# RWKV-7 mixer in a decoder step: preparation of a pair of heads split over two blocks, and the tensor engine's products kept in written order

## Chip, cores and metric

The kernel runs on one core of a Trainium2 chip. The metric is the device time of one execution in microseconds (us). The program is fully unrolled: there are no loops left on the chip, and each engine runs one fixed list of instructions.

## What is computed

One inference step of a two-layer decoder: 256 prompt tokens and 8 samples of 4 tokens, 288 columns in all. Layer 0 mixes with Mamba-2, layer 1 with RWKV-7; around each mixer stand two SwiGLU networks and a gate. The change is in the RWKV-7 mixer, whose core for each of 16 heads of width 64 is a recurrence over time:

```python
def step(S, inp):
    r_t, d_t, k_t, v_t, kk_t, a_t = inp
    sa = jnp.einsum('bhij,bhj->bhi', S, -kk_t)
    S = (S * d_t[:, :, None, :] + sa[..., None] * (kk_t * a_t)[:, :, None, :]
         + v_t[..., None] * k_t[:, :, None, :])
    return S, jnp.einsum('bhij,bhj->bhi', S, r_t)
```

Before it stand projections of the mixed rows (r, k, v, and low-rank ones for decay, a and the gate g), after it a group norm, a bonus term, the gate and the projection `w_o`.

## The kernel before

**Engines and weights.** Weights come from memory in units of 128x1024 (tile `raw`, issued on SP). Four 128x128 tiles at a time are split into a high part (`whi`, ACT, L55) and a low part (`wlo`, DVE, L56); the pool `wsp` holds 8 such pieces of each. A product of a weight tile with 288 columns is three matmuls (`mm3`, L147 to L149). The projection of k is one fp32 matmul a tile (L1134), recorded as two.

**Pairs and chunks.** The 16 heads are 8 pairs; a pair fills the 128 partitions. The tokens of a pair are 5 chunks of 64 columns: four of the prompt, one with the samples. Within a chunk the recurrence becomes a triangular system, which is inverted by levels.

**Three generators make the stage.** Each `yield` ends a step.

- `prep(p)`, 18 steps s1 to s18: s1 squares k and sums it over a head (L1228: two products with `ones_m`), exponentials of the summed decay; s2 scales k, r and kk into the tiles `BK` and `AR` (13 DVE operations, no matmul); s3 and s4 the products between tokens (`by_tokens`, L1265) into `AA` and `BKt`; s5 the matrices `N16`, `XT` and a transpose; s6 to s15 five levels of two steps each: `Z` (L1325), then `X` and `XT` (one or two groups of products in `mms`, L1309); s16 to s18 a refinement, whose result is `TT`. s16 is read by ACT (`X0`) and by DVE (`IX`, L1348).
- `chain(p)`, 17 steps c1 to c17: c1 the bonus (two products) and 16 products with the samples' states `S0` (L1383); c2 to c13 `solve`, `solved` and `state` for the four prompt chunks in turn, with the samples' chunk beside them in c5, c6, c8 (`masked`) and c10 (`samples`); c14 splits the output `y`; c15 and c16 are two products each with `center` and `ones_m` (group norm); c17 ends it.
- `bulk(p)` and `bulk2(p)`, the large products of a pair, in items: `bulk2` g (five matmuls), then v in eight items, then the transpose of v (`pv`, L1180); `bulk` the decay and a (`sw`, `sa`), then k in eight items and r in eight. 27 items in all.

**Blocks and rounds.** The stage is written as blocks p = 0 to 8. Block p runs `chain(p - 1)` and `prep(p)` in rounds; in each round every generator does one step, and then 1.45 items on average (`RATE`) come from `fill(p)`: `bulk2(p)` and `bulk(p + 1)`, at the start also the gate's first layer (`gates`), at the end products of `w_o`.

```python
        for p in range(KD + 1):
            gens, acc = [], 0.0
            bulk = fill(p)
            if p < KD:
                gens.append(w.prep(p))
            if p > 0:
                gens.insert(0, w.chain(p - 1))
```

**What sets the order.** When the program is built, a scheduler lays out each engine's list. It keeps data dependences and buffers, and by its own estimate of times it lets an instruction that is ready pass an earlier one of the same engine that is not. So the tensor engine's order is not the written one.

**Buffers.** PSUM has eight banks, dealt out in rings (`set_rings`): `main` [0, 1, 7] for the large products, `A` [2, 3] for `prep` and `pv`, `R` [4, 5] and `Y` [6] for `chain`. A new group of products takes the ring's next bank when that bank's readers have ended.

Of the kernel before, what the change touches and what calls it, by code (L numbers as in the profile page):

```python
# [78 lines left out]
class K:  # L79
    def __init__(self, tc, io):  # L80
        self.tc, self.nc, self.io = tc, tc.nc, io
        self.la_split, self.la_units = 16, 4
        self.lagged = []
        self.bg = []
        self.uid = 0
        self.ring_at = {}
        self.act_set, self.act_load, self.act_group = None, None, []
# [55 lines left out]

    def mm3(self, ps, w, x, start, stop):
        nc = self.nc
        (wh, wl), (xh, xl) = w, x
        nc.tensor.matmul(ps, wh, xh, start=start, stop=False)  # L147
        nc.tensor.matmul(ps, wh, xl, start=False, stop=False)  # L148
        nc.tensor.matmul(ps, wl, xh, start=False, stop=stop)  # L149
# [801 lines left out]
RATE = 1.45  # L951
# [42 lines left out]
class Rwkv:  # L994
# [50 lines left out]
    def lead(self, g, r):  # L1045

        nc, k, ws = self.nc, self.k, self.k.ws
        so = self.t("so", [P, KD, 9])
        pu, pw = k.bank("main")[:, :NT], k.bank("main")[:, :NT]
        k.renew(8, 16, F32)  # L1050
        hg = k.A[8:16]
        for kt in range(KD):
            k.act(hg[kt], k.h[kt], AF.Copy, scale=g[:, kt:kt + 1])
            w = k.wn.next_whole("r_wa1", kt, 0)
            nc.tensor.matmul(pu, w, hg[kt], start=kt == 0, stop=kt == KD - 1)
        for kt in range(KD):
            nc.vector.tensor_tensor(self.u[kt], hg[kt], r, ALU.mult)
        lw = k.tmp("s")
        nc.vector.tensor_tensor(lw, pu, r, ALU.mult)
        for kt in range(KD):  # L1060
            u, xx = self.u[kt], self.xx[kt]
            us, xs = s84(u[:, 256:288]), s84(xx[:, 256:288])
            nc.vector.tensor_tensor(xx[:, 1:288], u[:, 0:287], u[:, 1:288], ALU.subtract)
            nc.vector.tensor_tensor(xs[:, :, 0:1], k.sh[:, kt].rearrange("p (b o) -> p b o", o=1), us[:, :, 0:1],
                                    ALU.subtract)
            k.act(xx[:, 0:1], u[:, 0:1], AF.Copy, scale=-1.0)
            nc.tensor.matmul(pw, k.sc[kt], xx, start=kt == 0, stop=kt == KD - 1)
            k.act(so[:, kt, 0:1], u[:, 255:256], AF.Copy)
            k.act(so[:, kt, 1:9].rearrange("p (b o) -> p b o", o=1), us[:, :, 3:4], AF.Copy)
        nc.sync.dma_start(k.io["shift_o"], so)  # L1070
        nc.vector.tensor_tensor(lw, lw, pw, ALU.add)
        k.act(lw[0:64], lw[0:64], AF.Tanh)
        self.stack(self.lw, lw, slice(0, 64), slice(64, 128))
        self.stack(self.la, lw, slice(64, 128), slice(0, 64))

    def gates(self):

        nc, k = self.nc, self.k
        pg = [k.bank(n)[:, :NT] for n in "YR"]
        for kt in range(KD):  # L1080
            m = [None] * kt + [self.t("mg", bufs=2)]
            self.mix(5, kt, m)
            for i in range(2):
                nc.tensor.matmul(pg[i], k.wn.next_whole("r_g1", kt, i), m[kt], start=kt == 0, stop=kt == KD - 1)  # L1084
# [13 lines left out]
    def stacked(self, ps, w, x, start=True):  # L1098

        self.nc.tensor.matmul(ps, w[0], x, start=start, stop=False)  # L1100
        self.nc.tensor.matmul(ps, w[1], x, start=False, stop=True)
# [24 lines left out]
    def proj(self, n, i, x, p):  # L1126

        k, d = self.k, self.d[p]
        ps = k.bank("main")[:, :NT]
        for kt in range(KD):  # L1130
            if p == 0:
                self.mix(i, kt, x)
            if n == "k":
                self.nc.tensor.matmul(ps, k.wn.next_whole("r_wk", kt, p), x[kt], start=kt == 0, stop=kt == KD - 1)  # L1134
# [27 lines left out]
    def bulk2(self, p):  # L1162
# [6 lines left out]
        d["g"] = self.t("g", bufs=3)  # L1169
# [7 lines left out]
        for ch in range(5):  # L1177
            for h in range(2):
                rows = slice(64 * h, 64 * h + 64)
                nc.tensor.matmul(pv[rows, 64 * ch:64 * ch + 64], v[rows, 64 * ch:64 * ch + 64] if ch < 4 else V[rows],  # L1180
                                 self.I[rows], start=True, stop=True)
# [5 lines left out]
    def mm2(self, ps, m, hi, lo):  # L1187

        self.nc.tensor.matmul(ps, m, hi, start=True, stop=False)  # L1189
        self.nc.tensor.matmul(ps, m, lo, start=False, stop=True)  # L1190
# [8 lines left out]
    def pads(self):  # L1199
        self.AR = [self.t(f"AR{i}", [P, 5, 2, 64]) for i in range(2)]  # L1200
# [14 lines left out]
    def prep(self, p):  # L1215
# [4 lines left out]
        AR, BK = self.AR[p % 2], self.BK  # L1220
        d["S0"] = self.t("S0", [P, 8, 64], bufs=2)
        nc.sync.dma_start(d["S0"], k.io["wkv_in"][p])
# [25 lines left out]
        rk = d["rk"] = self.t("rk", bufs=2)  # L1248
# [8 lines left out]
        AA = d["AA"] = self.t("AA", [P, 2, 5, 128], bufs=2)  # L1257
        BKt = d["BKt"] = self.t("BKt", [P, 2, 5, 64], bufs=2)
        H = [(h, slice(64 * h, 64 * h + 64), slice(64 - 64 * h, 128 - 64 * h)) for h in range(2)]

        def by_tokens(ps, ch, o, n, rhs):

            for i in (1, 0):
                for h, rows, ro in H:
                    nc.tensor.matmul(ps[h][rows if i else ro, o:o + n], BK[rows, ch, i], rhs(rows), start=True, stop=True)  # L1265
# [21 lines left out]
        N16 = self.t("N16", [P, 5, 64], F16)  # L1287
# [12 lines left out]
        X, XT = [self.t(n, [P, 5, 64], F16, bufs=2) for n in ("X", "XT")]  # L1300
        nc.vector.tensor_tensor(XT, N16, lv(0, 5), ALU.mult)

        def mms(lhs, rhs, n=5):

            ps = k.bank("A")[:, :320].rearrange("p (c t) -> p c t", c=5)
            for ch in range(n):
                for h in range(2):
                    rows = slice(64 * h, 64 * h + 64)
                    nc.tensor.matmul(ps[rows, ch], lhs(ch)[rows], rhs(ch)[rows], start=True, stop=True)  # L1309
# [11 lines left out]
        for i in range(1, 6):  # L1321
            n = chunks(i)
            pz = mms(at(N16), at(X), n)
            Z = self.t("Z", [P, 5, 64], F16)
            nc.vector.tensor_tensor(Z[:, :n], pz, lv(i, n), ALU.mult)  # L1325
            yield
            if i < 5:
                px = mms(at(XT), at(Z), n)
                X2 = self.t("X", [P, 5, 64], F16, bufs=2)
                k.act(X2[:, :n], px, AF.Copy)  # L1330
            pt = mms(at(Z), at(XT), n)
            XT2 = self.t("XT", [P, 5, 64], F16, bufs=2)
            k.act(XT2[:, :n], pt, AF.Copy)
            X, XT = X2, XT2
            if i == 1:
                XTs = self.t("XTs", [P, 64], F16)
# [6 lines left out]

        ps = mms(full, eye)
# [6 lines left out]
        for ch in range(5):  # L1351
            for h in range(2):
                rows = slice(64 * h, 64 * h + 64)
                nc.tensor.matmul(ps[rows, ch], AA[rows, 1 - h, ch, 0:64], X0[rows, ch], start=True, stop=True)
# [9 lines left out]
    def chain(self, p):  # L1364
# [4 lines left out]
        AR, AA, BKt, SAV, TT, E1, S0 = self.AR[p % 2], d["AA"], d["BKt"], d["SAV"], d["TT"], d["E1"], d["S0"]  # L1369
# [11 lines left out]
        for b in range(8):  # L1381
            for h, rows, _ in H:
                nc.tensor.matmul(pq[rows, 8 * b:8 * b + 8], S0[rows, b], AR[rows, 4, 0, 8 * b:8 * b + 8], start=b == 0,  # L1383
# [6 lines left out]
        def solve(ch):  # L1390

            pr, S = k.bank("R"), st["S"]
            for h, rows, ro in H:
                if ch == 4:
                    nc.tensor.matmul(pr[ro, 0:64], q[rows], self.I[rows], start=True, stop=False)
                elif S is not None:
                    nc.tensor.matmul(pr[ro, 0:64], AR[rows, ch, 0], S[rows], start=True, stop=False)
            for h, rows, ro in H:
                nc.tensor.matmul(pr[ro, 0:64], AA[rows, h, ch, 0:64], SAV[rows, h, ch], start=ch < 4 and S is None,
                                 stop=True)  # L1400
            if ch < 4 and S is not None:
                for h, rows, _ in H:
                    nc.tensor.matmul(py[rows, 64 * ch:64 * ch + 64], S[rows], AR[rows, ch, 1], start=False, stop=True,
# [4 lines left out]
        def solved(ch):  # L1408
            ps, S, rhs = k.bank("R"), st["S"], st[ch]
            for h, rows, _ in H:  # L1410
                nc.tensor.matmul(ps[rows, 0:64], TT[rows, ch], rhs[rows], start=True, stop=True)
# [6 lines left out]
        def state(ch):  # L1418
# [3 lines left out]
            for h, rows, _ in H:  # L1422
                nc.tensor.matmul(ps[rows, 0:64], BKt[:, h, ch], SAV[:, h, ch], start=True, stop=True)  # L1423
# [6 lines left out]
            for h, rows, _ in H:  # L1430
                nc.tensor.matmul(o[rows], SAV[:, h, ch], AA[:, h, ch, 64:128], start=False, stop=True,
# [12 lines left out]
        def samples():  # L1444

            ps = k.bank("R")
            for h, rows, _ in H:
                nc.tensor.matmul(pq[rows], SAV[:, h, 4], AA[:, h, 4, 64:128], start=False, stop=True,
                                 skip_group_check=True)
            for h, rows, _ in H:  # L1450
                nc.tensor.matmul(ps[rows, :], BKt[:, h, 4], st["sv"][h].rearrange("p b i -> p (b i)"), start=True,  # L1451
# [42 lines left out]
def rwkv(k, g, g_next):  # L1494
# [3 lines left out]
    with k.tc.tile_pool(name="rwkv", bufs=1) as pool:  # L1498
# [6 lines left out]
        k.set_rings(main=[0, 1, 7], A=[2, 3], R=[4, 5], Y=[6])  # L1505
# [17 lines left out]
        def fill(p):  # L1523
# [11 lines left out]
            if p == KD:  # L1535
# [220 lines left out]
```

## Time and profile before

| what | value |
|---|---|
| median of 3 runs | 1533.58 us (1533.34 to 1533.81) |
| the profiled execution's own time | 1533.7 us |
| its span, first to last instruction | 1531.7 us |
| granted tensor-engine clock, mean | 0.996 |
| blocks of the RWKV stage | from about 985 to about 1285 us of the span |
| in them: PE, weight loads, DVE, ACT busy | 295.1, 223.8, 224.0, 191.0 of 300 us |

PE is the tensor engine's matmuls, PEld its weight loads, DVE the vector engine, ACT the scalar engine. A row of the timeline gives the start in us from the span's start, the duration, engine, line, operation, the tiles (out<-in), the shape and, with xN, how many like instructions were merged; a bracket at the end is idle time of the engine before it and what ended that. Matmuls are pipelined, so durations of neighbours overlap: the distance between starts tells what one costs.

### The profile page before, as it was taken

The numbers are of one execution on the slowest core, as the hardware profiler recorded it, in microseconds if no ns is written. First come the engines' busy times: TensorE is split into PE (matmuls) and PEld (weight loads), VectorE is DVE, ScalarE is ACT, GpSimd is POOL, SyncE is SP. The second block draws the span as 40 slices with busy tenths as digits, with TensorE's granted clock in tenths as the row PEclk, the third lists the DMA queues.
The fourth block names the chain that finished last, engine by engine and source line by source line (L and its number), as shares of the span: only waits on it lengthen the run. The fifth ranks groups of instructions, "written<-read, shape, count | busy, mean of one in ns | idle before, by whom it ended". The sixth has DMA issues, their size and how long they took to land.

```text
span 1531.7 us, 35590 instructions
## 1 busy us (share of the span) xinstructions
PE 1512.1 (99%) x14178; PEld 1420.4 (93%) x14178; DVE 1099.8 (72%) x2321; ACT 970.4 (63%) x2217; POOL 48.5 (3%) x145
## 2 busy tenths in 40 slices
PE   9999999999999999999999999999999999999997
PEld 9999999999999999999999999777677778999997
DVE  7666568999998666656876655887776778666666
ACT  7555458999996555555755554766666746555545
POOL 0000002112100000000000000100000000000000
PEclk9999999999999999999999999999999999999999
DMA  7555563776765555555555555532222225555551
GB/s 246 167 167 166 169 208 118 260 237 204 249 227 188 172 166 166 166 166 168 168 166 166 167 165 167 163 111 71 76 74 66 71 65 163 166 166 166 167 169 56
DMA packets 75574, 243.48 MB, mean 159 GB/s; under 512 B 11728, under 2 KB 16976, under 8 KB 75408
## 3 DMA queue, kind: packets, MB, share of 16 engines
q1 hardware_dynamic: 75408, 241.21, 49.4%
q8 instruction: 111, 1.82, 0.5%
q14 instruction: 55, 0.45, 0.1%
HBM read 226.54 MB, written 14.64 MB: 157 GB/s over the span
## 4 chain that ended last, share of the span: by engine, by line
PE 92%; DVE 4%; ACT 3%; DMA 1%; issue 1%; SPq 0%; POOL 0%; DVEq 0%; POOLq 0%; ACTq 0%
PE bank L147 26%; PE bank L149 26%; PE bank L148 25%; PE bank L1309 2%; PE bank L1134 1%; PE bank L772 1%; PE bank L1451 1%; PE bank L1423 1%; PE bank L776 1%; PE bank L768 1%; PE bank L1189 1%; DVE wlo L56 1%; PE bank L1383 1%; PE bank L1084 1%; PE bank L749 0%
## 5 line engine op out<-in xcount | busy, mean ns | idle before, releaser
L147 PE MATMUL bank<-act,whi 128*128 128x288 f32 x2760 | 823.2, 299 | 5.8 <-ACT act L138 3.9
L148 PE MATMUL bank<-act,whi 128*128 128x288 f32 x2760 | 819.6, 297 | 0.9 <-DVE act L156 0.9
L149 PE MATMUL bank<-act,wlo 128*128 128x288 f32 x2760 | 815.2, 296 | 0.1
L55 ACT ACTIVATE whi<-raw 128x512 fp32r<-128x512 f32 x754 | 472.3, 632 | 434.4 <-PE bank L148 422.7
L56 DVE TENSOR_TENSOR wlo<-raw,whi 128x512 fp32r<-128x512 f32 x754 | 515.4, 689 | 262.8 <-ACT whi L55 236.0
L147 PEld LDWEIGHTS bank<-act,whi 128*128 128x128 f32 x2760 | 517.6, 188 | 11.9 <-ACT act L138 5.5
L148 PEld LDWEIGHTS bank<-act,whi 128*128 128x128 f32 x2760 | 521.9, 189 | 5.9 <-DVE act L156 1.8
L149 PEld LDWEIGHTS bank<-act,wlo 128*128 128x128 f32 x2760 | 521.2, 189 | 2.8 <-DVE wlo L56 0.3
L147 PE MATMUL bank<-more,whi 128*128 128x288 f32 x192 | 56.7, 295 | 0.0
L148 PE MATMUL bank<-more,whi 128*128 128x288 f32 x192 | 56.5, 294 | 0.0
L149 PE MATMUL bank<-more,wlo 128*128 128x288 f32 x192 | 56.4, 294 | 0.0
L321 DVE TENSOR_TENSOR t<-bank,rstd 128x288 f32<-128x288 f32 x88 | 39.8, 456 | 23.0 <-PE bank L149 23.0
L324 DVE TENSOR_TENSOR u<-bank,s 128x288 f32<-128x288 f32 x88 | 39.8, 456 | 22.6 <-PE bank L149 22.6
L673 DVE SCALAR_TENSOR_TENSOR conv_a<-X,vec,conv_a 128x312 f32<-128x312 f32 x96 | 50.9, 534 | 3.8 <-ACT conv_a L138 3.4
L138 ACT ACTIVATE s<-t 128x288 f32<-128x288 f32 x104 | 45.8, 443 | 6.1 <-DVE t L366 3.5
L138 ACT ACTIVATE X<-bank 128x256 f32<-128x256 f32 (+2 forms) x98 | 30.7, 340 | 21.8 <-PE bank L1309 20.8
L138 ACT ACTIVATE act<-h,vec 128x288 fp32r<-128x288 f32 (+1 forms) x71 | 37.1, 528 | 7.4 <-DMA h<-in_xT 2.8
L1134 PE MATMUL bank<-act,raw 128*128 128x288 f32 x128 | 40.8, 434 | 0.0
L148 PEld LDWEIGHTS bank<-more,whi 128*128 128x128 f32 x192 | 36.3, 189 | 0.0
L149 PEld LDWEIGHTS bank<-more,wlo 128*128 128x128 f32 x192 | 36.2, 189 | 0.0
L147 PEld LDWEIGHTS bank<-more,whi 128*128 128x128 f32 x192 | 36.0, 187 | 0.0
L1325 DVE TENSOR_TENSOR Z<-bank,lv 128x256 f16<-128x256 f32 (+1 forms) x40 | 17.5, 437 | 24.0 <-PE bank L1309 23.5
(385 smaller groups left out, 1737.1 us busy)
## 6 DMA issues: line engine op xcount, KB each, us to landing
raw<-in_w SPq DMA_DIRECT2D x377, 512.0 KB, 3.6
h0a<-in_ssm_a SPq DMA_DIRECT2D x16, 512.0 KB, 5.7
h0b<-in_ssm_b SPq DMA_DIRECT2D x16, 512.0 KB, 5.1
out_ssm_s<-h0b SPq DMA_DIRECT2D x16, 512.0 KB, 4.3
raw<-in_wn SPq DMA_DIRECT2D x11, 512.0 KB, 3.5
S<-in_wkv_in SPq DMA_DIRECT2D x8, 256.0 KB, 3.9
out_wkv_s<-S SPq DMA_DIRECT2D x8, 256.0 KB, 2.0
h<-in_xT SPq DMA_DIRECT2D x8, 144.0 KB, 4.4
```

The source lines that it names most:

```text
L55: nc.scalar.activation(hi, src, AF.Copy)
L56: nc.vector.tensor_tensor(lo, src, hi.bitcast(F32), ALU.subtract)
L138: i = self.nc.scalar.activation(out, in_, func, **kw)
L147: nc.tensor.matmul(ps, wh, xh, start=start, stop=False)
L148: nc.tensor.matmul(ps, wh, xl, start=False, stop=False)
L149: nc.tensor.matmul(ps, wl, xh, start=False, stop=stop)
L321: nc.vector.tensor_tensor(t, pg, r, ALU.mult)
L324: nc.vector.tensor_tensor(u, pu, s, ALU.mult)
L673: nc.vector.scalar_tensor_tensor(a[:, :312], X[:, t:t + 312], k.g(f"conv_w{t}")[:, ct:ct + 1], a[:, :312], ALU.mult, ALU.add)
L1134: self.nc.tensor.matmul(ps, k.wn.next_whole("r_wk", kt, p), x[kt], start=kt == 0, stop=kt == KD - 1)
L1309: nc.tensor.matmul(ps[rows, ch], lhs(ch)[rows], rhs(ch)[rows], start=True, stop=True)
L1325: nc.vector.tensor_tensor(Z[:, :n], pz, lv(i, n), ALU.mult)
```

## The change

- A third pair is at work at once. `prep(p)` is cut in two: its first 9 steps (`HALF`) run in block p, the other 9 in block p + 1, and `chain(p)` runs in block p + 2. There are ten blocks, 0 to 9, and in a round the order is chain step, step of the older prep, step of the younger prep, items.
- From the first block to the last, each tensor-engine product goes through `K.mm`, which ties it behind the one written before it. The tie is for the scheduler alone: it puts no wait on the chip.
- `RATE` 1.45 becomes 1.6; `bulk2(p)` moves one block later.
- Rings: `main` [0, 1], `A` [2, 3, 7].
- Buffers: `AR`, `AA`, `BKt`, `rk` 3 instead of 2; `N16`, `Z` 2 instead of 1; `X`, `XT`, `XTs` one set for even and one for odd pairs; `mg` 1 instead of 2, `g` 2 instead of 3; `wsp` 6 instead of 8 for the whole kernel.
- The load of `S0` moves from s1 to s16.

```diff
+    def mm(self, *a, **kw):
+        i = self.nc.tensor.matmul(*a, **kw)
+        if self.kept is not None:
+            if self.kept:
+                self.after(i, self.kept[-1])
+            self.kept = [i]
+        return i
...
-RATE = 1.45
+RATE = 1.6
+HALF = 9
...
-            m = [None] * kt + [self.t("mg", bufs=2)]
+            m = [None] * kt + [self.t("mg", bufs=1)]
...
-        d["g"] = self.t("g", bufs=3)
+        d["g"] = self.t("g", bufs=2)
...
-        d["S0"] = self.t("S0", [P, 8, 64], bufs=2)
-        nc.sync.dma_start(d["S0"], k.io["wkv_in"][p])
...
+        d["S0"] = self.t("S0", [P, 8, 64], bufs=2)
+        nc.sync.dma_start(d["S0"], k.io["wkv_in"][p])
         ps = mms(full, eye)
...
-        k.set_rings(main=[0, 1, 7], A=[2, 3], R=[4, 5], Y=[6])
+        k.set_rings(main=[0, 1], A=[2, 3, 7], R=[4, 5], Y=[6])
...
-            if p < KD:
-                yield from w.bulk2(p)
+            if 0 < p <= KD:
+                yield from w.bulk2(p - 1)
             if p + 1 < KD:
                 yield from w.bulk(p + 1)
-            if p == KD - 1:
+            if p == KD:
...
-        for p in range(KD + 1):
+        preps = {}
+        k.kept = []
+        for p in range(KD + 2):
             gens, acc = [], 0.0
             bulk = fill(p)
+            if p > 1:
+                gens.append(w.chain(p - 2))
+            if 0 < p <= KD:
+                gens.append(preps.pop(p - 1))
             if p < KD:
-                gens.append(w.prep(p))
-            if p > 0:
-                gens.insert(0, w.chain(p - 1))
+                preps[p] = w.prep(p)
+                gens.append(itertools.islice(preps[p], HALF))
...
+        k.kept = None
...
-            tc.tile_pool(name="wsp", bufs=8) as k.wsp, \
+            tc.tile_pool(name="wsp", bufs=6) as k.wsp, \
```

More of the change, by code (lines that the diff above doesn't have):

```diff
@@ L1 @@
+import itertools
 import numpy as np
@@ L85, in __init__ @@
         self.uid = 0
+        self.kept = None
         self.ring_at = {}
@@ L1054, in lead @@
             w = k.wn.next_whole("r_wa1", kt, 0)
-            nc.tensor.matmul(pu, w, hg[kt], start=kt == 0, stop=kt == KD - 1)
+            k.mm(pu, w, hg[kt], start=kt == 0, stop=kt == KD - 1)
         for kt in range(KD):
@@ L1066, in lead @@
             k.act(xx[:, 0:1], u[:, 0:1], AF.Copy, scale=-1.0)
-            nc.tensor.matmul(pw, k.sc[kt], xx, start=kt == 0, stop=kt == KD - 1)
+            k.mm(pw, k.sc[kt], xx, start=kt == 0, stop=kt == KD - 1)
             k.act(so[:, kt, 0:1], u[:, 255:256], AF.Copy)
@@ L1098, in stacked @@
     def stacked(self, ps, w, x, start=True):
-        self.nc.tensor.matmul(ps, w[0], x, start=start, stop=False)
-        self.nc.tensor.matmul(ps, w[1], x, start=False, stop=True)
+        self.k.mm(ps, w[0], x, start=start, stop=False)
+        self.k.mm(ps, w[1], x, start=False, stop=True)
     def mix(self, i, kt, out):
@@ L1133, in proj @@
             if n == "k":
-                self.nc.tensor.matmul(ps, k.wn.next_whole("r_wk", kt, p), x[kt], start=kt == 0, stop=kt == KD - 1)
+                self.k.mm(ps, k.wn.next_whole("r_wk", kt, p), x[kt], start=kt == 0, stop=kt == KD - 1)
             else:
@@ L1179, in bulk2 @@
                 rows = slice(64 * h, 64 * h + 64)
-                nc.tensor.matmul(pv[rows, 64 * ch:64 * ch + 64], v[rows, 64 * ch:64 * ch + 64] if ch < 4 else V[rows],
+                k.mm(pv[rows, 64 * ch:64 * ch + 64], v[rows, 64 * ch:64 * ch + 64] if ch < 4 else V[rows],
                                  self.I[rows], start=True, stop=True)
@@ L1187, in mm2 @@
     def mm2(self, ps, m, hi, lo):
-        self.nc.tensor.matmul(ps, m, hi, start=True, stop=False)
-        self.nc.tensor.matmul(ps, m, lo, start=False, stop=True)
+        self.k.mm(ps, m, hi, start=True, stop=False)
+        self.k.mm(ps, m, lo, start=False, stop=True)
     def square(self, ps_in, hi, lo, sq):
@@ L1199, in pads @@
     def pads(self):
-        self.AR = [self.t(f"AR{i}", [P, 5, 2, 64]) for i in range(2)]
+        self.AR = [self.t(f"AR{i}", [P, 5, 2, 64]) for i in range(3)]
         self.BK = self.t("BK", [P, 5, 2, 64])
@@ L1255, in prep @@
         yield
-        AA = d["AA"] = self.t("AA", [P, 2, 5, 128], bufs=2)
-        BKt = d["BKt"] = self.t("BKt", [P, 2, 5, 64], bufs=2)
+        AA = d["AA"] = self.t("AA", [P, 2, 5, 128], bufs=3)
+        BKt = d["BKt"] = self.t("BKt", [P, 2, 5, 64], bufs=3)
         H = [(h, slice(64 * h, 64 * h + 64), slice(64 - 64 * h, 128 - 64 * h)) for h in range(2)]
@@ L1264, in by_tokens @@
                 for h, rows, ro in H:
-                    nc.tensor.matmul(ps[h][rows if i else ro, o:o + n], BK[rows, ch, i], rhs(rows), start=True, stop=True)
+                    k.mm(ps[h][rows if i else ro, o:o + n], BK[rows, ch, i], rhs(rows), start=True, stop=True)
         ps = [k.bank("A"), k.bank("A")]
@@ L1298, in lv @@
             return self.lv16[:, i:i + 1].to_broadcast([P, n, 64])
-        X, XT = [self.t(n, [P, 5, 64], F16, bufs=2) for n in ("X", "XT")]
+        tX, tXT, tXs = [f"{n}{p % 2}" for n in ("X", "XT", "XTs")]
+        X, XT = [self.t(n, [P, 5, 64], F16, bufs=2) for n in (tX, tXT)]
         nc.vector.tensor_tensor(XT, N16, lv(0, 5), ALU.mult)
@@ L1308, in mms @@
                     rows = slice(64 * h, 64 * h + 64)
-                    nc.tensor.matmul(ps[rows, ch], lhs(ch)[rows], rhs(ch)[rows], start=True, stop=True)
+                    k.mm(ps[rows, ch], lhs(ch)[rows], rhs(ch)[rows], start=True, stop=True)
             return ps[:, :n]
@@ L1335, in prep @@
             if i == 1:
-                XTs = self.t("XTs", [P, 64], F16)
+                XTs = self.t(tXs, [P, 64], F16)
                 k.act(XTs, XT[:, 4], AF.Copy)
@@ L1353, in prep @@
                 rows = slice(64 * h, 64 * h + 64)
-                nc.tensor.matmul(ps[rows, ch], AA[rows, 1 - h, ch, 0:64], X0[rows, ch], start=True, stop=True)
+                k.mm(ps[rows, ch], AA[rows, 1 - h, ch, 0:64], X0[rows, ch], start=True, stop=True)
         R = self.t("R", [P, 5, 64], F16)
@@ L1368, in chain @@
         col = slice(p, p + 1)
-        AR, AA, BKt, SAV, TT, E1, S0 = self.AR[p % 2], d["AA"], d["BKt"], d["SAV"], d["TT"], d["E1"], d["S0"]
+        AR, AA, BKt, SAV, TT, E1, S0 = self.AR[p % 3], d["AA"], d["BKt"], d["SAV"], d["TT"], d["E1"], d["S0"]
         H = [(h, slice(64 * h, 64 * h + 64), slice(64 - 64 * h, 128 - 64 * h)) for h in range(2)]
@@ L1382, in chain @@
             for h, rows, _ in H:
-                nc.tensor.matmul(pq[rows, 8 * b:8 * b + 8], S0[rows, b], AR[rows, 4, 0, 8 * b:8 * b + 8], start=b == 0,
+                k.mm(pq[rows, 8 * b:8 * b + 8], S0[rows, b], AR[rows, 4, 0, 8 * b:8 * b + 8], start=b == 0,
                                  stop=True, skip_group_check=b > 0)
@@ L1394, in solve @@
                 if ch == 4:
-                    nc.tensor.matmul(pr[ro, 0:64], q[rows], self.I[rows], start=True, stop=False)
+                    k.mm(pr[ro, 0:64], q[rows], self.I[rows], start=True, stop=False)
                 elif S is not None:
-                    nc.tensor.matmul(pr[ro, 0:64], AR[rows, ch, 0], S[rows], start=True, stop=False)
+                    k.mm(pr[ro, 0:64], AR[rows, ch, 0], S[rows], start=True, stop=False)
             for h, rows, ro in H:
-                nc.tensor.matmul(pr[ro, 0:64], AA[rows, h, ch, 0:64], SAV[rows, h, ch], start=ch < 4 and S is None,
+                k.mm(pr[ro, 0:64], AA[rows, h, ch, 0:64], SAV[rows, h, ch], start=ch < 4 and S is None,
                                  stop=True)
@@ L1402, in solve @@
                 for h, rows, _ in H:
-                    nc.tensor.matmul(py[rows, 64 * ch:64 * ch + 64], S[rows], AR[rows, ch, 1], start=False, stop=True,
+                    k.mm(py[rows, 64 * ch:64 * ch + 64], S[rows], AR[rows, ch, 1], start=False, stop=True,
                                      skip_group_check=True)
@@ L1410, in solved @@
             for h, rows, _ in H:
-                nc.tensor.matmul(ps[rows, 0:64], TT[rows, ch], rhs[rows], start=True, stop=True)
+                k.mm(ps[rows, 0:64], TT[rows, ch], rhs[rows], start=True, stop=True)
             nc.vector.tensor_copy(SAV[64:128, 0, ch], ps[64:128, 0:64])
@@ L1422, in state @@
             for h, rows, _ in H:
-                nc.tensor.matmul(ps[rows, 0:64], BKt[:, h, ch], SAV[:, h, ch], start=True, stop=True)
+                k.mm(ps[rows, 0:64], BKt[:, h, ch], SAV[:, h, ch], start=True, stop=True)
             S2 = self.t("S", [P, 64], bufs=2)
@@ L1430, in state @@
             for h, rows, _ in H:
-                nc.tensor.matmul(o[rows], SAV[:, h, ch], AA[:, h, ch, 64:128], start=False, stop=True,
+                k.mm(o[rows], SAV[:, h, ch], AA[:, h, ch, 64:128], start=False, stop=True,
                                  skip_group_check=True)
@@ L1447, in samples @@
             for h, rows, _ in H:
-                nc.tensor.matmul(pq[rows], SAV[:, h, 4], AA[:, h, 4, 64:128], start=False, stop=True,
+                k.mm(pq[rows], SAV[:, h, 4], AA[:, h, 4, 64:128], start=False, stop=True,
                                  skip_group_check=True)
             for h, rows, _ in H:
-                nc.tensor.matmul(ps[rows, :], BKt[:, h, 4], st["sv"][h].rearrange("p b i -> p (b i)"), start=True,
+                k.mm(ps[rows, :], BKt[:, h, 4], st["sv"][h].rearrange("p b i -> p (b i)"), start=True,
                                  stop=True)
```

23 lines of the change are left out of this document (11 added, 12 removed).

## The prediction

> **What bounds the kernel now.** I read the page first, then the busy times by stretch, then the timeline of one block, engine by engine.
>
> ```profile
> span 1531.7 us, 35590 instructions
> PE 1512.1 (99%) x14178; PEld 1420.4 (93%) x14178; DVE 1099.8 (72%) x2321; ACT 970.4 (63%) x2217; POOL 48.5 (3%) x145
> PE 92%; DVE 4%; ACT 3%; DMA 1%; issue 1%; SPq 0%; POOL 0%; DVEq 0%; POOLq 0%; ACTq 0%
> 1320.00:1360.00 40.00, 40.00 (x305) 40.00 (x304) 25.35 (x44) 20.90 (x38) 0.00 (x0) 1.00 0.53 161
> 985.00:1285.00 300.00, 295.05 (x4124) 223.81 (x4124) 223.96 (x600) 190.95 (x515) 0.00 (x0) 0.99 0.26 80
> ```
>
> The chain that ended last is 92% PE. Columns of the last two rows: stretch, length, busy PE, PEld, DVE, ACT, POOL, clock, DMA share, GB/s. In a feed-forward stretch weight loads are busy all the time, 305 products in 40 us, 0.131 us each. In the RWKV blocks they are busy 224 of 300 us although PE shows 295. What fills the difference is seen between starts:
>
> ```profile
> 1092.49 0.29 PE L147 MATMUL bank<-act,whi 128*128 128x288 f32 x1
> 1092.63 0.30 PE L148 MATMUL bank<-act,whi 128*128 128x288 f32 x1
> 1092.76 0.30 PE L149 MATMUL bank<-act,wlo 128*128 128x288 f32 x1
> ...
> 1088.01 1.04 PE L1383 MATMUL bank<-AR,S 64*64 64x8 f32 x29
> ...
> 1111.08 0.28 PE L1399 MATMUL bank<-SAV,AA 64*64 64x64 f32 x4
> 1111.29 0.40 PE L147 MATMUL bank<-act,whi 128*128 128x288 f32 x1
> 1111.53 0.29 PE L148 MATMUL bank<-act,whi 128*128 128x288 f32 x1
> 1111.75 0.34 PE L1309 MATMUL bank<-Z,XT 64*64 64x64 f16 x10
> ```
>
> Among themselves, large products start 0.133 us apart and small ones about 0.03. At 1111 two large ones stand between small ones. The four L1399 start until about 1111.14 (0.28 less one's 0.22), so small to small takes 0.61: 0.15 out of the small shape, 0.24 to the second large one, 0.22 into the small shape. Two large ones and a small start would be 0.30. A visit to the small shapes therefore costs 0.31 us over its own products. Counting in the timeline each small start behind a large one, the 4,124 products of the stage make 189 visits, about 22 a block of 33 us (1088 to 1121): 59 us of the stage. Against that, what starts come later than the quickest quarter of like pairs sums to 22 us. So PE is the bound, with little waiting; the price is the switching. [...]
>
> **Visits, counted from the program.** In written order one round's small steps stand together, so a round makes one visit. Block 0: rounds 3 to 9, 7. Block 1: 9 and one for `pv`. Blocks 2 to 7: c1 to c13 are small, 13, and `pv`, 14 each, 84. Block 8: 14. Block 9: 13. Sum 128 against 189, 61 fewer: -19 us. Chain and prep shapes now meet (64-column state products next to level products, about twice a block); I add 2 us. The products are the same in number and kind, and so are the DVE and ACT operations.
>
> **Waits that the written order makes.** Until now a step that isn't ready was passed by an item. In the changed program the next product written must wait, and everything behind it on PE does too. In before this is seen only in places:
>
> ```profile
> 1102.40 0.33 PE L1265 MATMUL bank<-AR,BK 64*64 64x64 f32 x4 [0.56 <-DVE AA L1271]
> ```
>
> There PE idles 0.56 us until `AA` frees a bank for s4, with large products still to do behind it. For each dependence that lies in consecutive steps I set the time it takes against the PE work that the written order puts between (the cover).
>
> s2, from the norm's second product to `BK`:
>
> ```profile
> 1093.89 0.30 PE L1190 MATMUL bank<-ql,ones_m 128*128 128x288 f32 x1
> 1094.37 0.45 DVE L1240 TENSOR_SCALAR s<-bank 128x288 f32<-128x288 f32 x1
> 1095.03 0.43 ACT L138 ACTIVATE s<-s 128x288 f32<-128x288 f32 x1
> 1095.49 0.54 ACT L138 ACTIVATE s<-s,lnb 128x288 f32<-128x288 f32 x1
> 1096.69 0.45 DVE L1251 TENSOR_TENSOR rs_q<-rs_q,s 128x288 f32<-128x288 f32 x1
> 1099.42 0.41 DVE L1211 TENSOR_TENSOR BK<-rs_q,ss 128x256 f32<-128x256 f32 x1
> 1099.76 0.18 DVE L1213 TENSOR_TENSOR BK<-rs_q,ss 128x32 f32<-128x32 f32 x1
> ```
>
> It took 6.05 us, with DVE's other work in between; its own links alone take 3.7 (0.34 for the product, 0.45, 0.46, 0.54, 0.42, two for `AR` 0.44, one more scaling of `rs_q` 0.42, the last two 0.51, and hand-overs). Cover from s1 to s3: g's five products 0.67 and the switch 0.22; `solve` 0.1, a level's 16 products 0.3, six large ones with their switches 1.1; `solved` and a level 0.25: 2.7. Wait 1.0 to 3.3; I take 1.9, somewhat nearer the short end, since BK's other half can be made early.
>
> s4 to s5, and the copies of a level:
>
> ```profile
> 1103.17 0.75 PE L1265 MATMUL bank<-r_const,BK 64*64 64x64 f32 x28
> 1104.47 0.49 DVE L1280 TENSOR_TENSOR AA<-bank,r_const 128x128 f32<-128x128 f32 x2
> 1104.79 0.77 ACT L138 ACTIVATE BKt<-bank 128x320 f32<-128x320 f32 x2 [1.20 <-DVE AA L1280]
> 1105.57 0.95 ACT L138 ACTIVATE N<-AA 64x320 f16<-64x320 f32 x2
> 1106.55 0.32 DVE L1291 TENSOR_TENSOR N<-N,I 128x320 f16<-128x320 f16 x1 [0.20 <-ACT N L138]
> 1106.92 0.31 DVE L1301 TENSOR_TENSOR XT<-N,lv 128x320 f16<-128x320 f16 x1
> 1112.14 0.44 ACT L138 ACTIVATE X<-bank 128x320 f16<-128x320 f32 x1 [2.30 <-PE bank L1309]
> ```
>
> From the last start of s4 (about 1103.64) to XT's end 3.6, 3.0 without the DVE queue; cover: two items 1.14, two solves 0.55, a level 0.13, together 1.85. Wait 1.2. In round 4 the ring `A` deals s4's second bank from the same round's `X` products; by the row at 1112.14 (its products began at 1111.75) that bank is free 0.83 after they began, and s4 is reached after 0.3: 0.6 (0.4 to 0.9).
>
> `pv` in round 7 gets the bank of s16:
>
> ```profile
> 1090.22 0.20 PE L1309 MATMUL bank<-I,XTs 64*64 64x64 f16 x2
> 1090.58 0.42 ACT L138 ACTIVATE t<-bank 128x320 f32<-128x320 f32 x1
> 1091.32 0.48 DVE L1348 TENSOR_TENSOR u<-r_const,bank 128x320 f32<-128x320 f32 x1
> ```
>
> ACT and DVE read it in turn: 1.3 us after s16 at the least, cover 0.3 (one step's level products). Wait 0.9 (0.7 to 1.5).
>
> The group norm:
>
> ```profile
> 1118.24 0.40 PE L1190 MATMUL bank<-cl,center 128*128 128x288 f32 x1
> 1119.05 0.41 ACT L138 ACTIVATE sq<-bank 128x288 f32<-128x288 f32 x1
> 1119.49 0.46 DVE L1197 TENSOR_TENSOR cl<-sq,ch 128x288 fp32r<-128x288 f32 x1 [0.71 <-ACT sq L138]
> 1120.00 0.40 PE L1190 MATMUL bank<-cl,ones_m 128*128 128x288 f32 x1
> 1121.30 0.46 DVE L1374 TENSOR_TENSOR cl<-rk,ch 128x288 fp32r<-128x288 f32 x1 [0.19 <-ACT ch L138]
> ```
>
> c15 to c16 takes 1.76; cover 1.06 (two items and two norm products): 0.7. c16 to the next c1 (the single `ch` and `cl`) 1.8, cover 1.46: 0.35. The other chain steps take 0.7 to 1.0, and rounds give 1.0 or more: nothing by themselves.
>
> Queues: in rounds 1 to 9 I add up some 17 us of DVE work (s2, AA, levels, s16 to s18, masks, gates, splits) on about 19 us of PE work, and in the rest 7 on 10.6. A DVE busy at 0.9 delays many links; I take 1.0 (0 to 4). A full block waits 1.9 + 1.2 + 0.6 + 0.9 + 0.7 + 0.35 + 1.0, about 6.7, with 0.3 left of before (`samples`) 7.0; bounds 4.3 and 10.5. Six full blocks: 42 (26 to 63). The ends: block 0, where `mg`'s one buffer makes mix, products, mix take turns in the double rounds, 5; block 1, where v's mixing meets s2, 6; blocks 8 and 9 about 5: 16 (9 to 24). Together 58 (35 to 87), less the 22 that go: +36.
>
> [...] If ready products could pass waiting ones, the 58 would vanish and the sum would be some -38 us (-19 + 2 - 22 + 1).
>
> **Edits of small price.** The split weights:
>
> ```profile
> L55 ACT ACTIVATE whi<-raw 128x512 fp32r<-128x512 f32 x754 | 472.3, 632 | 434.4 <-PE bank L148 422.7
> 225.00:235.00 10.00, 10.00 (x76) 9.77 (x74) 9.93 (x26) 6.20 (x14) 1.37 (x3) 1.00 0.64 242
> ```
>
> ACT waits 423 us for PE to free a piece: all 8 are full, and two fewer take 3.2 us (24 products) off that reserve. Where DVE is full (225 to 235, the way into Mamba) two pieces come 1.4 us later at most; with the way out of RWKV I take +1 (0 to 4). S0's load is issued eleven rounds ahead of its use, over 11 us, on an SP that issues little in the blocks: nothing; without that, its landing. `main` with two banks is covered by the 0.4 us copies a whole projection earlier; `g` with two is freed at c17 of the block before: nothing (up to 0.5 a block if a copy is late, in the queue term).
>
> **Sum.** -19 + 2 + 36 + 1 = +20. On the profiled execution's 1533.7 (span 1531.7 and 2.0 around it; the median, 1533.58, is 0.1 lower): 1553.6, 1.3% slower.
>
> **Rivals.**
> 1. *Covered waits: faster.* Three pairs give a step a whole round, and ACT and DVE can run ahead while only one small step a round is left (rounds 10 to 18); then s2 is half done at the border and the norm hidden. For: the weight loads' 224 of 300 and DVE at 0.75 of the stage. Against: mm2 of s1 has its place in round 1, and y to BK can't start earlier. Waits of 21 instead of 58: 1533.7 - 19 + 2 - 1 + 1, about 1517. It decides where all waits stay under 38 us, 4 a full block. [...]
> 2. *DVE becomes the bound of rounds 1 to 9: much slower.* Fixed lists on three engines wait for each other; 11 us a block: 66 + 20 - 22 - 19 + 3, +48, 1582. For: DVE's 17 of 19. Against: each PE wait lets DVE catch up.
> 3. *Nothing happens*: the scheduler's order was near the written one and pairs weren't short of time; visits stay at 180 or so, waits at 22: 1531 to 1536. Against: 22 visits a block where the written order of before has 18.
>
> **How the numbers follow.** Forecast 0.50, rival 1 0.27, rival 2 0.13, rival 3 0.10. What this kernel's measurement can tell from no change is 0.2%, 3 us. Slower 0.63, same 0.10, faster 0.27. The likeliest's own range, from the bounds of the waits, is 1530 to 1585, its bulk 1538 to 1572. For 8 in 10 the range reaches to the middle of rival 1 and of rival 2, which leaves out half of each, 0.2: 1517 to 1582.
>
> **What would show it.** In the blocks' timeline: visits near 128; a PE bracket or gap ahead of L1265 each block (BK, then X), of L1180, of L1190 with `ones_m`, and before L1309 behind XT; a block's period (from L1383 to L1383) of 36 us against 33.3; PEld's share of the stage lower; as many instructions. Wrong would be: a period under 33, gaps at s3 and s5 missing, DVE's s2 done before the block begins, or stalls at the way into Mamba above 4 us.

## The result and the profile after

The changed kernel takes 1601.06 us (median, 1600.85 to 1605.32) against 1533.52 us of the kernel before on the same chip: a ratio of 1.0443 [1.0431, 1.0456], 67 us slower. The direction was forecast; the size was 20 us, and the time lies above the range.

The page of the changed kernel, its head and the rows by slices for PE, weight loads and the clock:

```profile
span 1599.0 us, 35593 instructions
PE 1529.0 (96%) x14178; PEld 1440.1 (90%) x14178; DVE 1104.6 (69%) x2321; ACT 966.6 (60%) x2217; POOL 56.4 (4%) x146
...
PE   9999999999999999999999997888888889999997
PEld 8999998999999999999999996666666668999997
...
PEclk9999999999999999999999999888778789999999
```

The same 14,178 products; everything that changed stands in slices 25 to 33, where PE falls from 9 to 7 and 8, and from slice 26 on the granted clock with it. Busy times by stretch (columns as in the prediction: stretch, length, PE, weight loads, DVE, ACT, POOL, clock, DMA share, GB/s), first the blocks, then what follows them, in the changed kernel:

```profile
985.00:1352.00 367.00, 315.21 (x4147) 247.52 (x4146) 231.60 (x608) 194.41 (x526) 1.61 (x10) 0.84 0.22 66
1352.00:1599.00 247.00, 238.64 (x1803) 237.72 (x1801) 162.67 (x302) 134.94 (x248) 0.00 (x0) 0.99 0.48 152
```

and what follows them in the kernel before:

```profile
1285.00:1531.00 246.00, 238.96 (x1807) 238.11 (x1805) 161.86 (x300) 135.49 (x247) 0.00 (x0) 0.99 0.48 151
```

The blocks took 300 us and take 367; outside them nothing moved. In the blocks DVE is busy 232 of 367 us, 0.63, where it was 0.75. What PE waited for there, in the changed kernel (engine, line and what it waited for: us in total, times, longest; L149 is now the line of every product, because all go through `mm`):

```profile
PE bank L149 <- DVE AR L1225: 12.5, 6, 2.2
PE bank L149 <- DVE XT L1312: 8.7, 7, 1.5
PE bank L149 <- DVE rstd L1500: 6.6, 6, 1.6
PE bank L149 <- DVE u L1361: 4.6, 7, 0.7
PE bank L149 <- DVE mg L1119: 4.4, 5, 2.3
PE bank L149 <- DVE BK L1223: 3.9, 7, 0.9
PE bank L149 <- DVE cl L1209: 2.8, 8, 0.4
```

These are the places that the prediction named: `AR` and `BK` before s3, `XT` before s5, `u` before `pv`, the group norm, `mg`. But they come to 43.5 us (twelve smaller rows of the same view add 8), and the stage lost 67. Some of the rest is in the clock. The same view in short stretches of the changed kernel, cut where the clock changed (the second row is the end of the first):

```profile
1069.20:1099.90 30.70, 25.39 (x396) 19.42 (x391) 20.91 (x58) 20.33 (x56) 0.00 (x0) 1.00 0.23 72
1096.50:1099.90 3.40, 1.79 (x38) 1.48 (x33) 2.91 (x9) 2.45 (x7) 0.00 (x0) 1.00 0.02 5
1099.90:1110.20 10.30, 9.46 (x141) 7.61 (x141) 3.80 (x11) 2.59 (x7) 0.00 (x0) 0.50 0.16 52
1140.90:1154.60 13.70, 12.05 (x181) 10.14 (x180) 4.42 (x16) 3.98 (x11) 0.00 (x0) 0.50 0.01 2
1154.60:1175.00 20.40, 18.23 (x265) 13.48 (x261) 14.42 (x36) 14.64 (x42) 0.00 (x0) 1.00 0.31 89
1175.00:1178.40 3.40, 3.40 (x38) 3.02 (x33) 2.13 (x8) 1.16 (x4) 0.00 (x0) 0.51 0.25 104
1178.40:1181.90 3.50, 1.32 (x21) 0.98 (x19) 2.89 (x8) 1.40 (x4) 0.00 (x0) 0.99 0.18 20
1181.90:1202.30 20.40, 18.28 (x272) 15.24 (x270) 8.73 (x24) 8.28 (x24) 0.00 (x0) 0.50 0.07 24
```

For 115 of the 367 us the clock stands at one half (116 with the start of its first stretch, which lies ahead of 985); in the blocks of before it did so for about 7. The timeline of one block, changed kernel, PE alone (start, duration, operation, and in brackets the wait before it):

```profile
1173.41 0.40 PE L149 MATMUL bank<-ch,ones_m 128*128 128x288 f32 x1 [1.01 <-DVE rstd L1500]
...
1175.94 0.44 PE L149 MATMUL bank<-lgl,whi 128*128 128x288 f32 x1
1176.18 0.44 PE L149 MATMUL bank<-lgh,wlo 128*128 128x288 f32 x1
1176.42 0.44 PE L149 MATMUL bank<-lg,whi 128*128 128x288 f32 x1
...
1179.14 0.29 PE L149 MATMUL bank<-X,N 64*64 64x64 f16 x8
1181.62 0.49 PE L149 MATMUL bank<-AR,BK 64*64 64x128 f32 x4 [2.18 <-DVE AR L1225]
1182.58 1.97 PE L149 MATMUL bank<-AR,BK 64*64 64x128 f32 x28 [0.47 <-DVE BK L1223]
1192.49 0.47 PE L149 MATMUL bank<-I,XT 64*64 64x64 f16 x10 [1.13 <-DVE XT L1312]
1198.91 1.12 PE L149 MATMUL bank<-r_const,v 64*64 64x64 f32 x16 [0.53 <-DVE u L1361]
```

At 1176 the large products start 0.24 us apart instead of 0.133: the engine works at half speed just after one wait, until 1178.4. It is back at full clock for 3.4 us, in which it waits again (2.18 us, for `AR`), and at half from 1181.9 on, for 20.4 us.

**Where the 67 us are.** For every two neighbouring products of the blocks I took the distance between their starts. The bracketed waits are set apart. What is left has a mean for each kind of neighbours; large is a product of shape 128*128, small one of 64*64 or 128*64:

| mean distance without waits, us | large to large | large to small | small to large | small to small |
|---|---|---|---|---|
| before, full clock | 0.180 | 0.267 | 0.140 | 0.031 |
| after, full clock | 0.178 | 0.265 | 0.169 | 0.030 |
| after, half clock | 0.308 | 0.391 | 0.239 | 0.042 |

What the half clock adds is counted against the first row.

| in the blocks, us | before | after | difference | forecast of it |
|---|---|---|---|---|
| products and visits at full clock | 292 | 281 (113 visits for 189) | -11 | -17 |
| what the half clock adds to them | 3 | 34 | +31 | none |
| bracketed waits | 5 | 52 | +47 | +36 |
| sum | 300 | 367 | +67 | +19 |

At full clock, away from the waits, the products of the changed kernel start no later than before, but for the way out of the small shapes (2.5 us in all).

### The profile page after: what moved, and what is told of

Read it like the earlier page. It is cut to its first block, busy times and chain, and to the rows that moved or that the text cites. A ratio compares the mean times of both kernels' runs of the same rounds, so it can differ in the third digit from the quotient of the medians.

```text
span 1599.0 us, 35593 instructions
## 1 busy us (share of the span) xinstructions
PE 1529.0 (96%) x14178; PEld 1440.1 (90%) x14178; DVE 1104.6 (69%) x2321; ACT 966.6 (60%) x2217; POOL 56.4 (4%) x146
## 5 line engine op out<-in xcount | busy, mean ns | idle before, releaser
L149 PE MATMUL bank<-act,whi 128*128 128x288 f32 x5520 | 1128.3, 299 | 5.3 <-ACT whi L57 2.7
L149 PEld LDWEIGHTS bank<-act,whi 128*128 128x128 f32 x5520 | 891.3, 190 | 18.4 <-issue 3.6
L149 PE MATMUL bank<-act,wlo 128*128 128x288 f32 x2760 | 814.8, 296 | 0.1
L149 PEld LDWEIGHTS bank<-act,wlo 128*128 128x128 f32 x2760 | 524.6, 190 | 0.8 <-DVE wlo L58 0.3
L149 PE MATMUL bank<-more,whi 128*128 128x288 f32 x384 | 77.1, 295 | 0.0
L149 PEld LDWEIGHTS bank<-more,whi 128*128 128x128 f32 x384 | 61.4, 188 | 0.0
L149 PE MATMUL bank<-more,wlo 128*128 128x288 f32 x192 | 56.4, 294 | 0.0
L149 PE MATMUL bank<-act,raw 128*128 128x288 f32 x144 | 45.0, 441 | 1.3 <-DVE sw L1133 0.8
L149 PE MATMUL bank<-AR,BK 64*64 64x128 f32 (+1 forms) x320 | 26.4, 396 | 16.3 <-DVE AR L1225 12.5
L149 PEld LDWEIGHTS bank<-AR,BK 64*64 64x64 f32 x320 | 18.8, 208 | 21.8 <-issue 14.5
L149 PEld LDWEIGHTS bank<-act,raw 128*128 128x128 f32 x144 | 25.7, 196 | 12.1 <-issue 4.1
L149 PEld LDWEIGHTS bank<-more,wlo 128*128 128x128 f32 x192 | 36.2, 189 | 0.0
L141 ACT ACTIVATE SAV<-bank 64x64 f32<-64x64 f32 (+1 forms) x56 | 15.3, 275 | 33.8 <-DVE SAV L1425 29.8
```

Source lines behind the costliest of these rows:

```text
L141: i = self.nc.scalar.activation(out, in_, func, **kw)
L149: i = self.nc.tensor.matmul(*a, **kw)
```

## The experiments

**The tie or the third pair?** One kernel is the changed one without the tie, the other the kernel before with nothing but the tie.

```diff
 (changed kernel: e1_three_free)
-        k.kept = []
 (kernel before: e2_two_tied; every product of the stage through mm)
+        k.kept = []
         for p in range(KD + 1):
...
+        k.kept = None
```

> The changed kernel without the tie: three pairs, rings and buffers as changed, products in the scheduler's order. If the written order makes the loss (waits on PE, and the halved clock that follows them), the blocks come back to about 300 us, waits on PE to some 20 us, the clock to 1.00, and the time lies between 1520 and 1540 us. If three pairs themselves make it (crowded DVE, ring A shared by two preparations, main with two banks), the tie is not what matters: 1570 us or more.

> The kernel before with the tie alone: two pairs, RATE 1.45, its rings and buffers. If the written order makes the loss, it shows here at least as strongly, since fewer steps lie between a step and the next one of the same pair: waits at BK, XT and the group norm in each block, half clock in between, 1570 to 1630 us. If three pairs make it, the tie alone costs little: 1530 to 1545 us.

Without the tie: 1535.43 us, 1.0012 [1.0003, 1.0021]. The tie alone: 1607.0 us, 1.0476 [1.0460, 1.0491]. Blocks of the first, then of the second with its largest waits:

```profile
985.00:1285.00 300.00, 290.31 (x4135) 223.64 (x4134) 227.13 (x606) 194.95 (x524) 0.21 (x2) 0.99 0.26 82
```

```profile
985.00:1358.00 373.00, 308.11 (x4120) 237.97 (x4121) 227.77 (x598) 190.32 (x515) 0.00 (x0) 0.89 0.20 64
```

```profile
PE bank L147 <- DVE AR L1222: 18.9, 7, 2.8
PE bank L147 <- DVE XT L1310: 14.7, 8, 3.0
PE bank L147 <- ACT SAV L139: 7.2, 6, 1.2
```

So the tie makes the whole loss; the third pair, the rings and the buffers together cost about 2 us. Where the order is tied, the third pair with its rings, buffers and `RATE` lightens the loss only a little: `AR` 12.5 for 18.9, `XT` 8.7 for 14.7, and about 6 us in all.

**What does the halved clock cost by itself?** Keep the waits, but give PE something to do in them: 16 products ahead of s3's and 8 ahead of s5's, written to columns that nothing reads. It stands in six of the eight pairs, from the first chain on.

```diff
+    def filler(self, n):
+        for _ in range(n):
+            self.k.mm(pz[:, 320:448], self.ones_m, self.ones_m, start=False, stop=True, ...)
...
+        self.filler(16)     # ahead of s3's products
+        self.filler(8)      # ahead of s5's
```

> The changed kernel with products that nobody reads (16 of 128x128x128 ahead of the products of s3, 8 ahead of those of s5, into unused columns of the chain's bank), where PE waits longest. If waits lower the clock and the lower clock is a cost of its own (about 28 us of products at half rate, counted from the starts), the time at half clock falls from 116 us to under 60 and the time by 10 to 25 us, to 1576 to 1591 us, though work was added. If the clock isn't decided by these waits, the added work costs 0 to 12 us: 1601 to 1613 us.

1581.77 us, 1.0311 [1.0294, 1.0327]: 19 us less than the changed kernel, by adding work. Its blocks:

```profile
985.00:1330.00 345.00, 308.51 (x4287) 243.81 (x4286) 230.23 (x605) 193.84 (x525) 0.48 (x4) 0.93 0.22 71
```

Time at half clock falls from 116 to 48 us. The filler brings no `BK` or `XT` forward: from the last product that is used to the first of s3 there are 14.3 us in all, in the changed kernel and with the filler, and ahead of s5 12.5 and 13.7. So about 19 of the 67 us go with the clock: 0.28 us for each of the 68 us at half clock that were avoided. Counted from the starts, the half clock adds 16 us there instead of 34, which is nearly the same step. (The 28 us of the expectation are a narrower count of the 34.)

**Were s3 and s5 reached too early?** Empty rounds, in which `prep` does nothing while the others go on: two between s2 and s3, one between s4 and s5.

```diff
-HALF = 9
+HALF = 12
...
+        yield        # twice, between s2 and s3
+        yield
...
+        yield        # between s4 and s5
```

> The changed kernel with two empty rounds after s2 and one after s4, HALF 12 in place of 9: more written work between the steps that wait longest, nothing else changed. If the covers decide, the waits for AR and BK (16 us) and for XT (9 us) fall below 5 us together, half clock below 60 us, and the time comes to 1555 to 1578 us. If DVE's throughput in the blocks decides, the waits move to other steps and the time stays at 1592 to 1606 us.

1565.92 us, 1.0208 [1.0191, 1.0225]. Waits of that kernel:

```profile
PE bank L149 <- DVE XT L1315: 13.1, 8, 5.0
PE bank L149 <- DVE rstd L1503: 6.8, 7, 1.6
PE bank L149 <- ACT BKt L141: 5.8, 6, 1.1
PE bank L149 <- DVE BK L1223: 1.3, 5, 0.3
```

The wait at s3 went from 16.4 us to 1.3, the clock's half time to 61, and the time fell as expected. But `XT`, expected to fall too, did not follow. One round was too little for it, one wait of 5.0 is new, and `pv`, which takes its bank from the same ring, now waits for `BKt`. A step that is put later makes room at one place and meets other owners of the bank at the next.

**Which bank holds up c1?** The prediction put the wait between c16 and the next c1 down to the single buffers `ch` and `cl`. The view says `rstd`, which c17 computes from the bank that c15 filled; that bank is the next of ring `R`, and c1 asks for it. The edit moves the bonus of c1 into c9 and `pv` to ring `R`.

```diff
-        pv = k.bank("A")
+        pv = k.bank("R")
...
-        pr = k.bank("R")[:, :NT]          (in c1, with the bonus)
...
+                if ch == 2 and n == 1:    (c9)
+                    bonus()
```

> The changed kernel with two groups given other banks: the bonus of c1 is computed in c9 (its bank of ring R then no longer waits for the group norm's last reader), and pv takes its bank from ring R in place of A. If these two waits are waits for banks, they go (in the changed kernel 6.6 us behind rstd and 4.6 us behind u), the clock stays up a little longer, and the time falls by 10 to 22 us, to 1579 to 1591 us. If they only stand where PE would wait anyway (for DVE, for the next step), the time stays within 5 us of 1601.

1576.61 us, 1.0278 [1.0263, 1.0294], 2 us below what was expected, and among the waits `rstd` and `u` are gone:

```profile
PE bank L149 <- DVE AR L1225: 14.4, 6, 2.4
PE bank L149 <- DVE XT L1312: 10.9, 7, 2.7
PE bank L149 <- DVE BK L1223: 6.2, 7, 1.2
PE bank L149 <- DVE mg L1119: 4.5, 5, 2.3
```

11.2 us of waits are taken away, 6.5 come back at the others, and the time falls by 24 us, more than either: the half clock falls from 116 to 65 us. By the accounting above, about 4 us are waits, 12 the clock, and 8 products that start closer together.

**All of it together.** `e6_all` joins the two edits, with two empty rounds at each of the two places, one between c15 and c16, `mg` with two buffers and `RATE` 1.51. `e7_all3` has three rounds instead of two.

```diff
-RATE = 1.6
-HALF = 9
+RATE = 1.51
+HALF = 13            (15 with three rounds)
...
+        yield        (two, then three, after s2 and after s4)
+        yield
...
+        yield        (between c15 and c16)
```

> The changed kernel with the banks of e5, two empty rounds after s2 and two after s4, one between c15 and c16, mg with two buffers and RATE 1.51. If the covers are the whole matter, waits on PE come to 20 us or less, the clock stays at 1.00 but for the first microseconds, and the fewer visits (113 in place of 189) show: 1515 to 1530 us, faster than before. If the written order can't do without waits because DVE and ACT are too full, 1540 to 1560 us.

> As e6 with three empty rounds after s2 and after s4. By the covers: no slower than e6, within 5 us. By full engines: the later rounds get the preparation's work on top of the group norm, and the time is 5 to 15 us above e6.

1551.97 us, 1.0116 [1.0095, 1.0136], a miss: it was expected under the kernel before. And 1537.28 us, 1.0032 [1.0020, 1.0044], 15 us below that, where at most 5 were expected from one more round. Waits of the first, then of the second:

```profile
PE bank L149 <- DVE XT L1316: 10.7, 7, 4.5
PE bank L149 <- ACT v L141: 7.6, 8, 1.2
PE bank L149 <- DVE sw L1133: 3.5, 8, 0.9
```

```profile
PE bank L149 <- ACT SAV L141: 6.3, 11, 1.0
PE bank L149 <- DVE AA L1284: 4.8, 12, 0.8
PE bank L149 <- DVE XT L1318: 3.5, 1, 3.5
```

With three rounds `XT` waits once, at the start, instead of seven times. The links now have the room that they need.

**The small buffers by themselves**: the kernel before with `wsp` 6, `mg` 1, `g` 2.

```diff
-            tc.tile_pool(name="wsp", bufs=8) as k.wsp, \
+            tc.tile_pool(name="wsp", bufs=6) as k.wsp, \
```

> The kernel before with the smaller buffers alone: 6 split pieces in place of 8, mg 1 in place of 2, g 2 in place of 3. By the prediction's price 0 to 6 us, 1534 to 1540 us, seen on the way into Mamba. The rival is that the scheduler's order needs them: 1545 us or more.

1532.63 us, 0.9997 [0.9988, 1.0007]: they cost nothing where the order is free.

**The first blocks without the tie, and the tail.** In `e9_start_free` the tie of `e7_all3` begins at block 2. `e10_wo_early` also moves the products of 15 weight tiles of `w_o` from block 8 into block 7, and of 12 from block 9 into block 8; `e12_tail` slows the items in block 9 as well.

```diff
-        k.kept = []
         for p in range(KD + 2):
+            if p == 2:
+                k.kept = []
...
-            if p == KD:
+            if p == KD - 1:
+                    yield from wo(mo, range(KD - 3))   (e10, e12)
...
-                acc += RATE
+                acc += RATE if p <= KD else 1.1        (e12 alone)
```

> e7 (three empty rounds after s2 and s4, other banks for bonus and pv) with the tie from block 2 on: blocks 0 and 1, where one pair or two are at work and v and the gate are still mixed, keep the scheduler's order. If what e7 has lost against before lies in those blocks (its later blocks take 30.7 us where before takes 32.5), 5 to 10 us go: 1527 to 1533 us, as fast as before or a little faster. If the loss is at the end (block 7 has ten items in place of 27), nothing changes: 1535 to 1540 us.

> e9 with fifteen products of w_o moved from block 8 into block 7, whose rounds have no large products left and where the clock was halved for 10 us in e7. If cover is what is missing there, the half clock of block 7 goes and the time is 3 to 7 us below e9. If the rows of the output that they need come too late, it is the same within 2 us.

> e10 with 1.1 items a round in block 9, so that about five products of w_o are left when the last chain ends, where PE waited 3.5 us for the first product of the next network and the clock was halved for 7 us. If it is that end that eats what block 7 gained, 2 to 5 us go: 1523 to 1527 us. If the chain of block 9 loses cover for it, 1528 to 1532 us.

1528.32 us, 0.9973 [0.9962, 0.9984]: a kernel tied from block 2 on, 5 us below the kernel before. The other two are 1528.80 and 1529.68 us, 0.9967 [0.9956, 0.9979] and 0.9962 [0.9948, 0.9976], no different from it. With the products moved, block 7's half clock, 10 us in `e7_all3`, is gone, but a new wait stands at the stage's end with 7 us of half clock about it:

```profile
PE bank L149 <- ACT act L141: 3.5, 1, 3.5
```

On the tail the two runs decide nothing.

**The new schedule without the tie.** If the written order is what gained, the schedule of `e7_all3` must lose when the tie is taken from it.

```diff
 (e7_all3, giving e11_spread_free)
-        k.kept = []
```

> e7's schedule (empty rounds, banks, RATE 1.51, three pairs) with no tie at all: the scheduler's order. If the written order, once its waits are covered, is what gains (fewer visits, blocks of 30.7 us), this is slower than e9: 1531 to 1537 us. If the longer rounds and the banks gain by themselves, it is as fast as e9 or faster: 1524 to 1530 us.

1526.67 us, 0.9961 [0.9947, 0.9975]: as fast as the best tied one. The blocks of it (in its profiled execution, the slowest of six with 1531.89 us), then those of `e9_start_free`, whole and in three steady blocks:

```profile
985.00:1277.00 292.00, 284.52 (x4104) 217.93 (x4103) 220.68 (x590) 189.21 (x516) 1.45 (x5) 0.97 0.24 77
1080.00:1200.00 120.00, 117.86 (x1907) 88.94 (x1907) 93.77 (x259) 82.86 (x235) 0.00 (x0) 1.00 0.23 72
```

```profile
985.00:1277.00 292.00, 273.47 (x4129) 213.06 (x4128) 226.32 (x600) 191.24 (x522) 1.39 (x5) 0.98 0.26 82
1080.00:1200.00 120.00, 110.91 (x1922) 84.93 (x1922) 94.91 (x258) 83.12 (x235) 0.00 (x0) 1.00 0.23 73
```

The free order makes 180 visits and keeps PE busy 118 of 120 us. The tied one makes 138 and idles 9 of 120. Both take 30.7 us a steady block, against 32.5 in the kernel before and 31.3 in `e1_three_free`, which loses that gain again at the ends of the stage. So what gains is the schedule: the third pair, the place of the steps and of the banks, `mg` and `RATE`, whose shares the runs do not part. The order gains nothing on top of it. By the accounting above, products and visits at full clock take 269 us in the tied kernel and 278 in the free one, bracketed waits 18 and 8: the visits that the order saves come back as waits.

## Why the prediction was right and wrong

**Right: the direction and its mechanism.** The visits fell as the count from the program said, and further (113, forecast 128). With e1 and e2 it is shown that the written order is what makes PE wait, and the two largest waits are those that were worked out from link and cover:

| wait in the changed kernel | forecast, us each | measured |
|---|---|---|
| s2 to s3 (`AR` and `BK`) | 1.9 (1.0 to 3.3) | 16.4 in 7 blocks, 2.3 |
| s4 to s5 (`XT`) | 1.2 | 8.7 in 7, 1.2 |
| `pv` behind s16 (`u`) | 0.9 | 4.6 in 7, 0.7 |
| `mg`, block 0 | 5 in all | 4.4 |
| c15 to c16 (`cl`) | 0.7 | 2.8 in 8, 0.35 |
| c16 to c1 | 0.35 | 6.6 in 6, 1.1 (`rstd`) |
| ring `A` at s4 | 0.6 | none |

The wait at c1 had the wrong owner: by the view it is a bank and not a tile, since `rstd` reads the bank of ring `R` that c1 takes next. The wait goes with the bonus in e5; that edit takes the tiles `ch` and `cl` out of c1 as well, so by itself it doesn't part the two.

**Wrong: the sum took each microsecond of waiting as a microsecond, at a clock that stays.** That is the step that failed. It read a clock of 1.00 and 0.99 in the rows of the kernel before and carried it over to a kernel whose PE would idle a fifth of some stretches; no term of the sum is a clock term. Measured, the half clock adds 31 us by starts, and e3 shows about 19 of them without making the waits ahead of s3 and s5 shorter. At e3's price of 0.28 us, the 109 us more at half clock come to 31 as well. This term alone takes the forecast to 1585 us, past its range. In the trace the stretches at half clock are 3.4, 6.8, 10.2, 13.7 and 20.5 us long, and in them 0.24 us stands between the starts of large products where 0.133 stood.

**Mis-sized: what the waits replace.** Forecast were 58 us of waits, of them 1.0 us a block for the queues, less 22 us of lateness that would go. Measured are 52 us of bracketed waits. So the waits themselves were a little less than forecast, with some luck: ring `A` and c15 to c16 waited less, c1 and s3 more. But in the kernel before only 5 us were waits of this kind, so that 5 went and not 22. That makes +47 in place of +36, which alone would have left the time inside the range.

**The other terms.** The visits fell further than forecast and still brought less, 11 us for 17. By the means above, a visit costs 0.20 us over its own products (0.267 + 0.140 - 0.180 - 0.031; 0.24 with the quick 0.133 for 0.180) and not the 0.31 of the one place that the prediction read, and 23 large products more fall into the longer window. The 2 us added for chain and prep shapes that meet were the author's estimate, and no run shows them: in the blocks a product of 64*64 and one of 128*64 follow one another 17 times in the changed kernel, 48 times in the kernel before. Nothing changed at the way into Mamba or elsewhere outside the blocks (forecast +1, measured 0, and e8 the same). Against the forecast, then: clock +31, waits +11, visits +6, `wsp` -1, which makes the 20 into 67.

**The rivals.** That DVE becomes the bound is refuted: from 1056 to 1293 us no 10 us have it busy more than 0.83, where in the kernel before it reached 0.96 (1056 to 1250 us). That the waits are covered was wrong for this kernel, where they are 52 and not under 38; e7 and e9 show what it would have taken, three empty rounds after s2 and after s4, and other banks. That nothing happens is what e1 measures: three pairs without the tie.

**The signs named ahead.** A block's period was forecast at 36 us and is 37.1 to 42.9 in the six full blocks; the brackets stand ahead of s3, s5, `pv` and the norm, but not ahead of s4.

## What to carry to other kernels

Where a change makes an engine keep a written order, list for every pair of consecutive steps the time of the links between them and the work written in between, banks included. Write a step as many rounds behind its source as the links need. A free scheduler may do as well by itself, as it did here. On the tensor engine, price a wait with the clock as well: here a stage with 52 us of waits stood at half clock for 115 of its 367 us, and each us at half clock cost 0.28 to 0.30 us more for the products. Products that nobody reads were cheaper here than an idle wait (by 19 us), but moving the steps and the banks won more (64 us in `e7_all3`).

## What the hardware showed that was not expected

The clock stood at one half for 115 of 367 us though the longest wait was 2.3 us (the `mg` row): it swung without any longer gap in PE's work.

What came ahead of its changes can be counted in the traces of the kernel before and of the changed one. In both, each stretch between two changes of the clock is 3.413 us long or a multiple of that, up to 536 us. I cut PE's busy time from 975 us to the end of the blocks into windows of that length, in step with the changes. After a window at full clock with PE busy less than half of it (0.28 to 0.45), the clock was halved 6 times of 6; with 0.50 to 0.75, 9 times of 18; with more, not once in 141. It came back to full 15 times, each time after a window with 0.90 or more, though not after each such window. The window from 1178.4 us holds the wait of 2.18 us: PE is busy 1.32 of 3.50 us in the row above, and the 20 us behind it were at half. From 1069 to 1096 the windows had 0.57 to 1.00 and the clock stayed; the next had 1.79 of 3.40 us, and the 10 us behind it were at half. The busy time of PE is modelled in the profile, and these are counts from two executions; what moves the clock they do not show.

The tied and the free kernel with the same schedule both stand at 30.7 us a steady block, though PE is busy 111 of 120 us in one and 118 in the other. No engine is full in the tied one (DVE 95, ACT 83 of 120), so what bounds it is probably a chain of links; which one was not settled. The times of these last kernels also spread more than those of the kernel before, 1524.7 to 1531.9 us for the free one. The clock goes with it: its two longest executions have a mean clock of 0.991, its three shortest 0.996 to 0.998. Why the clock falls in one execution and not in the next stays open.
